# Sparse attention's top-k: the lower 16 bits of each threshold read from eight sorted values, with a branch to the bit search; two changes of queue order

## The chip, the cores and the metric

One core of one Trainium2 chip runs the whole program. The metric is the device time of one execution in microseconds. Matmuls run on TensorE (PE), the other work on VectorE (DVE), ScalarE (ACT) and GpSimd (POOL); SyncE (SP) and POOL issue the transfers between HBM and the on-chip memory. Each engine takes its instructions strictly in the order of its own queue, and semaphores join the queues.

## What is computed

Two layers over 1040 tokens (16 learned ones ahead of 1024) of width 1024: a mixer with a residual add, then a SwiGLU FFN. Layer 0 mixes by gated linear attention, layer 1 by sparse attention, cut here to what matters:

```python
def attend(args):                                   # 128 queries
    s_idx = einsum('bqhd,bsd->bqhs', qib, k_idx) * IDX_DIM ** -0.5
    score = einsum('bqhs,bqh->bqs', relu(s_idx), wb)       # the indexer: 8 heads of 64
    score = where(admissible[None], score, -inf)           # chunk-causal
    top_val, top_idx = lax.top_k(score, n_sel)             # n_sel = 256
    c_sel = c[top_idx]                                     # 256-wide latents
    q_lat = einsum('bqhd,hcd->bqhc', qb, w_uk)             # 8 heads of 128
    logits = einsum('bqhc,bqkc->bhqk', q_lat, c_sel) * ATT_HEAD_DIM ** -0.5 + bias
    u = einsum('bhqk,bqkc->bqhc', softmax(where(valid, logits, -inf)), c_sel)
    return einsum('bqhc,hcd->bqhd', u, w_uv)
```

All is float32. `lax.top_k` takes the earlier key among equal scores.

## The kernel before

A product of float32 operands is three matmuls (`mm3`, L230 to L232) of parts that `split` makes: a rounded high part (`xh`, a cast on ACT, L225) and the rest (`xl`, a subtraction on DVE or POOL, L226). Names like `xh`, `wl`, `cth` in rows are such parts.

**Top-k.** The kernel gathers no keys: it finds for each of 1024 queries the 256th largest score and adds a mask to the logits. The scores `sc` (L915 to L924) stand with 128 queries on the partitions in eight blocks of up to 1040 keys; block 0 needs no search, and blocks 7, 1, 4, 3 and 5, 2, 6 form the two groups of `GROUPS`. The threshold is found bit by bit: a score's float bits, made monotone, are two 16-bit halves. `rounds(15)` counts on the upper half, one bit in a step: for each block one instruction counts the keys below `cand` (three blocks on ACT, L1102, four on DVE, L1105), and four small POOL instructions in `decide` (L1114 to L1118) set the next `cand`. `turnover` then leaves in the mask's buffer the lower half of the keys whose upper half equals the threshold's, and 0 for the rest; its count (L1175) is of the keys above. `rounds(16)` searches the lower half in the same way, then `th` (L1165 to L1142) puts the bits back, and seven steps write the mask: L1207 to L1214, with a prefix sum (L1209) for the ties.

**What sets the order.** `topk` is a generator, and its steps are spread over `units` (L955 on), PE's work beside it: nine units of the latents (projection L1024, root L279, `turn` L1038 to transpose them), then queries `(hd, c)` of eight heads by three stretches of tokens (344, 344, 336), keys, values. `costs` weighs each step, and after every unit so many steps are emitted as their weights have earned. `later.at(d, f)` puts `f` off by `d` ticks, and each unit ends with one tick. After this, attention starts: POOL adds the mask to the bias (L1275), PE makes logits, DVE the softmax sums (L1290).

**Ahead of the indexer.** The last FFN group of layer 0 ends with `second`: for its last tokens five partial products (`EARLY`, on the first half of the hidden rows) are made before the eight whole ones, whose results are added to `h` (L728). `ended` gives the norm's root to `later` (L833); its row mean on PE is L323. Then `dsa` makes index keys (ps of 344), index queries of two stretches (384 and 512 wide, four pairs of heads `e`) and transposes of the head weights (L935).

## Time and profile before

| what | value |
|---|---|
| runs | 2595.59, 2597.05, 2598.44 us (median 2597.05) |
| profiled execution | 2597.97 us, its span 2596.2 us |
| granted TensorE clock over the span | 0.985 |

The rows below come from the profiled execution, its times counted from the start of the span. "Busy" is time in which an engine ran an instruction; a releaser in brackets is what ended the idle time before it. [...] Rows of DVE and ACT of consecutive instructions can overlap by some hundredths.

### The profile page before, as it was taken

Reading aid. Unit: us, or ns where it says so; the run is one execution under the profiler, and the core shown is the slowest. Engines: PE = TensorE matmul, PEld = TensorE weight load, DVE = VectorE, ACT = ScalarE, POOL = GpSimd, SP = SyncE. Lnnn points to the kernel's source line nnn. Section 1 sums busy time; section 2 is a strip of 40 time slices with the busy share of each in tenths; the row PEclk is TensorE's granted clock in tenths of the full one; section 3 lists DMA queues with packets and bytes.
Section 4 is the critical chain, followed back from the end, with each engine's and each line's share of the span. In section 5 each row is a group of like instructions: output and inputs, shape, how many; then the busy total and the mean of one; then the engine's idle time right before and its main releaser. Section 6 shows DMA issues by size and latency. Waiting matters only on the chain.

```text
span 2596.2 us, 37989 instructions
## 1 busy us (share of the span) xinstructions
PE 2515.9 (97%) x15096; PEld 2334.5 (90%) x15096; DVE 1356.1 (52%) x2904; ACT 955.3 (37%) x1972; POOL 382.2 (15%) x587
## 2 busy tenths in 40 slices
PE   7999999999999999999898969999999999999997
PEld 6999999999999999999878959999988888888887
DVE  7575566643333334444679997762633333333336
ACT  5764453521111111112568867761511111111114
POOL 3000000111111111110203455440200000000001
PEclk9999999999999999999899979999999999999999
DMA  3113013123333333332311101122111111111111
GB/s 119 41 35 108 26 49 115 33 86 122 122 115 117 111 122 110 112 116 72 111 65 53 63 25 42 64 95 86 39 60 49 49 49 49 49 42 41 48 49 66
DMA packets 68788, 190.00 MB, mean 73 GB/s; under 512 B 7065, under 2 KB 18609, under 8 KB 65794
## 3 DMA queue, kind: packets, MB, share of 16 engines
q1 hardware_dynamic: 62642, 154.31, 17.9%
q0 software_dynamic: 5968, 33.26, 3.8%
q8 instruction: 118, 1.93, 0.3%
q14 instruction: 60, 0.49, 0.1%
HBM read 150.74 MB, written 41.58 MB: 74 GB/s over the span
## 4 chain that ended last, share of the span: by engine, by line
PE 40%; DVE 6%; issue 2%; ACT 2%; POOL 1%; DMA 0%; POOLq 0%; ACTq 0%; DVEq 0%
PE ps L231 12%; PE ps L232 12%; PE ps L230 12%; DVE jd L1105 2%; PE ps L1322 1%; DVE sc L924 1%; PE ps L1334 1%; PE ps L915 1%; POOL xl L226 0%; PE ps L917 0%; DVE pre L1209 0%; DVE no L342 0%; PE ps L1310 0%; ACT L330 0%; DVE h L342 0%
## 5 line engine op out<-in xcount | busy, mean ns | idle before, releaser
L230 PE MATMUL ps<-xh,wh 128*128 128x344 f32 (+6 forms) x2808 | 945.5, 337 | 1.9 <-DMA wh<-s_qidx_h 1.2
L231 PE MATMUL ps<-xl,wh 128*128 128x344 f32 (+6 forms) x2808 | 941.6, 335 | 1.0 <-POOL xl L226 0.6
L232 PE MATMUL ps<-xh,wl 128*128 128x344 f32 (+6 forms) x2808 | 940.1, 335 | 1.9 <-DVE wl L197 1.9
L230 PEld LDWEIGHTS ps<-xh,wh 128*128 128x128 f32 x2808 | 528.5, 188 | 32.4 <-DMA wh<-s_qidx_h 1.3
L231 PEld LDWEIGHTS ps<-xl,wh 128*128 128x128 f32 x2808 | 528.8, 188 | 30.1 <-DVE xl L226 1.0
L232 PEld LDWEIGHTS ps<-xh,wl 128*128 128x128 f32 x2808 | 528.8, 188 | 29.2 <-DVE wl L197 2.5
L715 DVE TENSOR_TENSOR t<-sg,ps 128x344 f32<-128x344 f32 (+4 forms) x116 | 65.1, 562 | 639.6 <-PE ps L232 637.9
L192 ACT CAST wh<-wraw 128x1056 fp32r<-128x1056 f32 (+2 forms) x160 | 163.9, 1049 | 581.1 <-PE ps L231 573.3
L728 DVE TENSOR_TENSOR h<-h,ps 128x344 f32<-128x344 f32 (+3 forms) x456 | 251.1, 567 | 163.9 <-PE ps L232 163.7
L230 PE MATMUL ps<-hh,wh 128*128 128x512 f32 (+2 forms) x800 | 280.3, 350 | 0.0
L231 PE MATMUL ps<-hl,wh 128*128 128x512 f32 (+2 forms) x800 | 280.0, 350 | 0.0
L232 PE MATMUL ps<-hh,wl 128*128 128x512 f32 (+2 forms) x800 | 279.8, 350 | 0.0
L197 DVE TENSOR_TENSOR wl<-wraw,wh 128x1056 fp32r<-128x1056 f32 (+2 forms) x158 | 192.1, 1238 | 72.3 <-ACT wh L192 70.5
L230 PE MATMUL ps<-wh,xh 128*128 128x256 f32 (+9 forms) x560 | 174.4, 311 | 9.4 <-ACT xh L225 5.0
L232 PE MATMUL ps<-wh,xl 128*128 128x256 f32 (+9 forms) x560 | 169.6, 303 | 4.3 <-DVE xl L226 2.3
L714 ACT ACTIVATE sg<-ps 128x344 f32<-128x344 f32 (+4 forms) x116 | 57.8, 498 | 300.6 <-PE ps L232 295.6
L231 PE MATMUL ps<-wl,xh 128*128 128x256 f32 (+9 forms) x560 | 167.7, 299 | 0.0
L225 ACT CAST hh<-t 128x344 fp32r<-128x344 f32 (+4 forms) x116 | 60.0, 517 | 285.2 <-DVE t L715 285.2
L230 PEld LDWEIGHTS ps<-hh,wh 128*128 128x128 f32 x800 | 150.0, 188 | 14.6
L231 PEld LDWEIGHTS ps<-hl,wh 128*128 128x128 f32 x800 | 150.3, 188 | 14.3
L232 PEld LDWEIGHTS ps<-hh,wl 128*128 128x128 f32 x800 | 150.5, 188 | 13.9
L230 PEld LDWEIGHTS ps<-wh,xh 128*128 128x128 f32 x560 | 110.9, 198 | 15.5 <-ACT xh L225 5.6
(289 smaller groups left out, 3390.1 us busy)
## 6 DMA issues: line engine op xcount, KB each, us to landing
wraw<-in_w_fi SPq DMA_DIRECT2D x44, 528.0 KB, 3.9
wraw<-in_w_fi SPq DMA_DIRECT2D x44, 496.0 KB, 4.9
wraw<-in_w_fo SPq DMA_DIRECT2D x22, 528.0 KB, 3.9
wraw<-in_w_fo SPq DMA_DIRECT2D x22, 496.0 KB, 5.0
s_skew<-s_rel POOLq DMA_DIRECT2D x8, 583.5 KB, 13.7
h<-in_ht SPq DMA_DIRECT2D x8, 520.0 KB, 5.1
wraw<-s_skew SPq DMA_DIRECT2D x8, 520.0 KB, 3.5
sg<-in_w_dq SPq DMA_DIRECT2D x16, 256.0 KB, 4.1
```

The costliest lines, as they stand in the source:

```text
L192: nc.scalar.copy(hi[:, a:e], r[:, : e - a])
L197: self.wlow.tensor_sub(lo[:, c:d], r[:, c - a : d - a], hi[:, c:d].bitcast(F32))
L225: self.nc.scalar.copy(hi, src)
L230: mm(p, sh, mh, start=first, stop=False, skip_group_check=True)
L231: mm(p, sh, ml, start=False, stop=False, skip_group_check=True)
L232: mm(p, sl, mh, start=False, stop=last, skip_group_check=True)
L714: nc.scalar.activation(sg[:, :n], pg[:, :n], AF.Silu)
L715: v.tensor_mul(t[:, :n], sg[:, :n], pu[:, :n])
L728: v.tensor_add(self.h[:, d, a : a + n], self.h[:, d, a : a + n], p[:, :n])
L915: nc.tensor.matmul(p, qx[:, hd, t], kxh[:, s0 : s0 + n], start=True, stop=False)
L924: eng.scalar_tensor_tensor(o, rt, wx[:, b, hd : hd + 1], o, op0=OP.mult, op1=OP.add)
L1105: v.tensor_scalar(j[:, :n], mu(b), cand, None, op0=OP.is_lt, op1=OP.add, accum_out=out)
```

## The change

1. **Top-k.** `rounds(16)` goes. `turnover` counts by ACT sign counts (7 of them, L1201) in place of DVE's seven counts, takes the eight largest lower halves of each block (`v.max`, seven instructions), works out each row's rank among the equal keys, and picks the value of that rank by a mask over eight places. `worst` is the largest rank of all rows; a 1x1 matmul (L1251) sums over the partitions whether any rank is above 7.5, a flag goes to DVE's register (L1254), and DVE branches (L1256): with the flag set it runs `search`, the 16 bits on DVE alone; otherwise it jumps over it. `If` puts an unconditional branch on every other engine at that place.
2. **Costs.** The list of step weights is 66 times 1.7 before; now 32 times 1.7, two of 6, one of 3. The mask steps keep theirs.
3. **Latents.** `turn` is put off by two more ticks.
4. **Index queries.** The 512-wide ones of `e` 0 and 1 come ahead of the head weights' transposes and of the 384-wide ones of `e` 2 and 3 (those of 0 and 1 are made earlier, among the keys).
5. **FFN.** One more tick after the five early products, and the root of the last but one stretch put off by 3 ticks for 2.
6. Rows 0 to 63 of block 1 get a mask of zeros at the end (their 272 keys less the inadmissible are 208 and fewer than 256, all taken).

```diff
@@ -756,6 +756,7 @@
...
                                 done[e] = out(hh, hl, wo, e, *cs[c], qs=[0])
+                            later.tick()
@@ -829,7 +830,7 @@
...
-                self.later.at(2 if a == last_chunks[-2][0] else 1, rstd)
+                self.later.at(3 if a == last_chunks[-2][0] else 1, rstd)
@@ -926,18 +927,26 @@
...
+                def head_weights():
+                    p = self.ps()
+                    for b in range(8):
+                        a = META + 128 * b
+                        nc.tensor.transpose(p[:, b * 64 : b * 64 + 64], wt[64:128, a : a + 128],
+                                            self.ident[64:128, 64:128])
+                    v.tensor_scalar(wx, p.rearrange("p (b c) -> p b c", b=8)[:, :, 0:8], 8 ** -0.5,
+                                    0.125, op0=OP.mult, op1=OP.mult)
...
+                for e in range(2):
+                    index_queries(144, 384, e)
+                index_queries(528, 512, 0)
+                index_queries(528, 512, 1)
+                head_weights()
+                for e in range(2, 4):
+                    index_queries(144, 384, e)
                 for e in range(4):
-                    index_queries(144, 384, e)
-                    if e == 0:
...
-                for e in range(4):
-                    index_queries(528, 512, e)
+                    if e > 1:
+                        index_queries(528, 512, e)
@@ -952,7 +961,7 @@
...
-                costs = [1.7] * 66 + [MASK] * 8
+                costs = [1.7] * 32 + [6.0] * 2 + [3.0] + [MASK] * 8
@@ -1029,7 +1038,7 @@
...
-                self.later.at(3 + i % 3, lambda i=i, c=c: turn(i, c))
+                self.later.at(5 + i % 3, lambda i=i, c=c: turn(i, c))
@@ -1083,11 +1094,17 @@
...
+        place = pool.tile([128, 8], F32, name="place")
+        for i in range(8):
+            v.memset(place[:, i : i + 1], float(i))
+        worst = pool.tile([128, 2], F32, name="worst")
+        flag = pool.tile([1, 1], I32, name="flag")
@@ -1154,6 +1171,11 @@
...
+            for c, b in enumerate(g["b"]):
+                n = nkeys(b)
+                v.tensor_scalar(g["rest"][:, c : c + 1], g["thr"][:, c : c + 1], -0.5 if c < g["na"] else -1.0,
+                                -1.0 if c < g["na"] else n / 2 - 1.0, op0=OP.mult, op1=OP.add)
@@ -1166,33 +1188,74 @@
...
-        def turnover(g):
-            cand = g["cand"]
-            for c in list(range(g["na"], g["n"])) + list(range(g["na"])):
+        def turnover(g, j):
+            cand, n, na, x, rank = g["cand"], g["n"], g["na"], g["x"], g["rank"]
+            top = pool.tile([128, n, 8], U16, name="top%d" % j)
+            tops = pool.tile([128, n, 8], F32, name="tops%d" % j)
+            v.tensor_scalar_add(x, cand, 0.5)
+            for c in range(n - 1, -1, -1):
                 b = g["b"][c]
-                n, tc = nkeys(b), cand[:, c : c + 1]
-                j = pool.tile([128, T], BF16, name="jd", tag="pre", bufs=2)
-                v.tensor_scalar(j[:, :n], mu(b), tc, None, op0=OP.is_gt, op1=OP.add,
-                                accum_out=g["cnt"][:, c : c + 1])
-                low = pool.tile([128, T], U16, name="low", tag="sg", bufs=2)[:, :n]
+                m, tc = nkeys(b), cand[:, c : c + 1]
+                t = pool.tile([128, T], BF16, name="jd", tag="pre", bufs=2)
+                nc.scalar.activation(t[:, :m], mu(b), AF.Sign, bias=x[:, c : c + 1], scale=-1.0,
+                                     accum_out=g["cnt"][:, c : c + 1])
+                low = pool.tile([128, T], U16, name="low", tag="sg", bufs=2)[:, :m]
                 nc.scalar.activation(low, half(b, 0), AF.Identity, bias=g["add"][:, c : c + 1],
                                      scale=g["sgn"][:, c : c + 1])
                 v.scalar_tensor_tensor(mu(b), mu(b), tc, low, op0=OP.is_equal, op1=OP.mult)
-            more(g, g["cnt"])
+                v.max(out=top[:, c, :], in_=mu(b))
             bits_of(g, 1)
-            start(g, 16)
+            v.scalar_tensor_tensor(rank, g["cnt"], 0.5, g["rest"], op0=OP.mult, op1=OP.add)
+            if 1 in g["b"]:
+                v.memset(rank[0:64, g["b"].index(1) : g["b"].index(1) + 1], 0.0)
+            v.tensor_reduce(worst[:, j : j + 1], rank, axis=mybir.AxisListType.X, op=OP.max)
+            for c in range(n):
+                v.tensor_scalar(tops[:, c, :], place, rank[:, c : c + 1], None, op0=OP.is_equal)
+            v.tensor_tensor(tops, tops, top, op=OP.mult)
+            v.tensor_reduce(cand, tops, axis=mybir.AxisListType.X, op=OP.max)
+        def search():
+            for g in groups:
+                thr, cand, below, flip = g["thr"], g["cand"], g["below"], g["flip"]
+                for c, b in enumerate(g["b"]):
+                    v.tensor_scalar(thr[:, c : c + 1], g["rank"][:, c : c + 1], -1.0, nkeys(b) - 1.0,
+                                    op0=OP.mult, op1=OP.add)
+                start(g, 16)
+                for bit in range(15, -1, -1):
+                    for c, b in enumerate(g["b"]):
+                        n = nkeys(b)
+                        t = pool.tile([128, T], BF16, name="jd", tag="pre", bufs=2)
+                        v.tensor_scalar(t[:, :n], mu(b), cand[:, c : c + 1], None, op0=OP.is_lt,
+                                        op1=OP.add, accum_out=g["cnt"][:, c : c + 1])
+                    v.tensor_sub(below, g["cnt"], thr)
+                    v.tensor_scalar(below, below, 0.0, -(2.0 ** bit), op0=OP.is_gt, op1=OP.mult)
+                    v.tensor_add(cand, below, flip)
+                    if bit:
+                        v.tensor_scalar_add(flip, cand, 2.0 ** (bit - 2) if bit > 1 else 0.5)
         for g in groups:
             signs(g)
             yield
         yield from rounds(15)
+        for j, g in enumerate(groups):
+            decide(g, 0)
+            turnover(g, j)
+            yield
+        v.tensor_reduce(worst[:, 0:1], worst, axis=mybir.AxisListType.X, op=OP.max)
+        v.tensor_scalar(worst[:, 0:1], worst[:, 0:1], 7.5, None, op0=OP.is_gt)
+        p = self.ps()
+        nc.tensor.matmul(p[0:1, 0:1], worst[:, 0:1], self.mean[:, 0:1], start=True, stop=True)
+        v.tensor_scalar(flag, p[0:1, 0:1], 0.0, None, op0=OP.is_gt)
+        yield
+        many = nc.values_load(flag, engines=[mybir.EngineType.DVE], min_val=0, max_val=1,
+                              skip_runtime_bounds_check_because="a comparison gives zero or one")
+        with self.tc.If(many > 0):
+            search()
         for g in groups:
-            decide(g, 0)
-            turnover(g)
-            yield
-        yield from rounds(16)
-        for g in groups:
-            decide(g, 0)
             bits_of(g, 0)
             clamp(g, g["th"].bitcast(F32))
...
+            if b == 1:
+                v.memset(mk(b)[0:64, :], 0.0)
```

What the change moves, by the order of instructions (before and after are apart; a bracket names the engines or transfer queues waited for).

**PE at the indexer's begin**, the last index key product and what follows it, before:

```order
7946 L231 MATMUL ps<-xl,wh 128x344 [waits Pool_49]
7947 L232 MATMUL ps<-xh,wl 128x344
7948 L935 MATMUL ps<-ident,wt 128x64 [waits DMAHW2_49,DMAHW3_49,DMAHW0_49,DMAHW5_49,PE_49,Activation_49]
7949 L935 MATMUL ps<-ident,wt 128x64
7950 L935 MATMUL ps<-ident,wt 128x64 [waits Activation_49]
7951 L935 MATMUL ps<-ident,wt 128x64 x2
7952 L935 MATMUL ps<-ident,wt 128x64 [waits Activation_49]
7953 L935 MATMUL ps<-ident,wt 128x64 x2
7954 L230 MATMUL ps<-xh,wh 128x384 [waits DMASW2_49]
7955 L231 MATMUL ps<-xl,wh 128x384
```

Now, with 45 more matmuls of width 512 above these rows (48 in all between the keys and the transposes):

```order
7993 L230 MATMUL ps<-xh,wh 128x512
7994 L231 MATMUL ps<-xl,wh 128x512
7995 L232 MATMUL ps<-xh,wl 128x512
7996 L934 MATMUL ps<-ident,wt 128x64 [waits DMAHW2_49,DMAHW3_49,DMAHW0_49,DMAHW5_49,PE_49,Activation_49]
7997 L934 MATMUL ps<-ident,wt 128x64
7998 L934 MATMUL ps<-ident,wt 128x64 [waits Activation_49]
7999 L934 MATMUL ps<-ident,wt 128x64 x2
8000 L934 MATMUL ps<-ident,wt 128x64 [waits Activation_49]
8001 L934 MATMUL ps<-ident,wt 128x64 x2
8002 L230 MATMUL ps<-xh,wh 128x384 [waits DMASW2_49,DVE_49]
8003 L231 MATMUL ps<-xl,wh 128x384
```

The transposes of `wt` and the 384-wide products, which wait for a load (DMASW), have moved behind 48 matmuls of width 512 that wait for nothing.

**PE in the latents**, the last of 96 matmuls of width 256 and the first transposes, before, and the last of 144 now:

```order
8414 L230 MATMUL ps<-wh,xh 128x256
8415 L231 MATMUL ps<-wl,xh 128x256
8416 L232 MATMUL ps<-wh,xl 128x256
8417 L1038 MATMUL ps<-ident,qf 128x16 [waits DVE_49,Activation_49]
8418 L1038 MATMUL ps<-ident,qf 128x16
8419 L230 MATMUL ps<-wh,xh 128x256 [waits Activation_49]
```

```order
8463 L230 MATMUL ps<-wh,xh 128x256
8464 L231 MATMUL ps<-wl,xh 128x256
8465 L232 MATMUL ps<-wh,xl 128x256
8466 L1047 MATMUL ps<-ident,qf 128x16 [waits DVE_49,Activation_49]
8467 L1047 MATMUL ps<-ident,qf 128x16
8468 L230 MATMUL ps<-wh,xh 128x256 [waits PE_49]
```

Two more units of 24 matmuls stand ahead of the first transposes. **ACT at the same place**, the last mask of `signs` and the root of the latents' norm, before and now:

```order
787 L1159 ACTIVATE mask<-sc,add_13507,sgn_13506 128x784
788 L1102 ACTIVATE ja,cnt_13481<-mask,cand_13485 128x1040 [waits Activation_49]
789 L1102 ACTIVATE ja,cnt_13481<-mask,cand_13485 128x272 [waits Activation_49]
790 L279 ACT_TABLE_LOAD
791 L279 ACTIVATE rs<-rs 128x3 [waits DVE_49]
792 L1102 ACTIVATE ja,cnt_13500<-mask,cand_13504 128x784 [waits Activation_49]
793 L1102 ACTIVATE ja,cnt_13481<-mask,cand_13485 128x1040 [waits Activation_49,Pool_49]
```

```order
786 L1181 ACTIVATE mask<-sc,add_13520,sgn_13519 128x784
787 L279 ACT_TABLE_LOAD
788 L279 ACTIVATE rs<-rs 128x3 [waits DVE_49]
789 L1119 ACTIVATE ja,cnt_13492<-mask,cand_13496 128x1040 [waits Activation_49]
790 L1119 ACTIVATE ja,cnt_13492<-mask,cand_13496 128x272 [waits Activation_49]
791 L1033 ACTIVATE qf,css<-ps 128x256 [waits PE_49]
792 L1119 ACTIVATE ja,cnt_13513<-mask,cand_13517 128x784 [waits Activation_49]
```

The root has moved ahead of two counts.

**PE in the queries** now, the end of unit (6,1) and the begin of (7,1); ahead of these rows stand the 72 matmuls of (6,0), (7,0) and (6,1), after them 24 of (7,1), 48 of width 336, then keys:

```order
9033 L230 MATMUL ps<-xh,wh 128x344
9034 L231 MATMUL ps<-xl,wh 128x344
9035 L232 MATMUL ps<-xh,wl 128x344
9036 L1251 MATMUL ps<-mean,worst 1x1 [waits DMAHW3_49,DMAHW4_49,DMAHW2_49,DMAHW6_49,DMAHW1_49,DMAHW7_49,DVE_49,Activation_49]
9037 L230 MATMUL ps<-xh,wh 128x344 [waits Activation_49]
9038 L231 MATMUL ps<-xl,wh 128x344
9039 L1256 UNCONDITIONAL_BRANCH
9040 L232 MATMUL ps<-xh,wl 128x344
```

**DVE at the thresholds**, the end of the search before, and now, with the rows of `search` (L1225 to L1236) between:

```order
1522 L226 TENSOR_TENSOR xl<-qf,xh 128x3x344 [waits Activation_49]
1523 L1105 TENSOR_SCALAR jd,cnt_13500<-mask,cand_13504 128x400 [waits DVE_49,Pool_49]
1524 L1105 TENSOR_SCALAR jd,cnt_13500<-mask,cand_13504 128x912 [waits DVE_49]
1525 L1165 TENSOR_TENSOR cand_13485<-cand_13485,sgn_13487 128x4 [waits Activation_49,Pool_49]
1526 L1166 TENSOR_TENSOR cand_13485<-cand_13485,add_13488 128x4 [waits DVE_49]
1527 L1167 CAST th_13489<-cand_13485 128x4 [waits DVE_49]
1528 L1140 SCALAR_TENSOR_TENSOR x_13490<-th_13489 128x4 [waits DVE_49]
1529 L1141 TENSOR_SCALAR y_13491<-x_13490 128x4 [waits DVE_49]
1530 L1142 TENSOR_TENSOR th_13489<-th_13489,y_13491 128x4 [waits DVE_49]
1531 L1165 TENSOR_TENSOR cand_13504<-cand_13504,sgn_13506 128x3 [waits Activation_49,Pool_49]
1532 L1064 SCALAR_TENSOR_TENSOR xl<-ps,xh 128x336 [waits Activation_49] x2
```

```order
1472 L1249 TENSOR_SCALAR worst<-worst 128x1 [waits DVE_49]
1473 L1218 TENSOR_REDUCE cand_13517<-tops_14766 128x3 [waits DVE_49]
1474 L226 TENSOR_TENSOR xl<-qf,xh 128x3x344 [waits Activation_49]
1475 L1073 SCALAR_TENSOR_TENSOR xl<-ps,xh 128x344 [waits Activation_49] x2
1476 L1252 TENSOR_SCALAR flag<-ps 1x1 [waits PE_49]
1477 L1254 TENSOR_LOAD flag [waits DMAHW3_49,DMAHW2_49,DMAHW4_49,DMAHW1_49,DMAHW5_49,DMAHW0_49,DMAHW6_49,DVE_49,DMAHW7_49,Activation_49,Pool_49]
1478 L1256 COMPARE_AND_BRANCH
1479 L1225 TENSOR_SCALAR thr_13494<-rank_13503 128x1 x4
1723 L1236 TENSOR_TENSOR cand_13517<-below_13516,flip_13518 128x3 [waits DVE_49]
1724 L1256 UNCONDITIONAL_BRANCH
1725 L1256 UNCONDITIONAL_BRANCH [waits DVE_49]
1726 L1187 TENSOR_TENSOR cand_13496<-cand_13496,sgn_13498 128x4 [waits DVE_49]
```

The thresholds (`cand` to `th`) followed the last decision of POOL; now they follow the branch, and so do the parts of the second stretch of queries (`xl` from `qf`), which stood ahead of them.

## Rows read from the trace of the kernel before

**Rows 1.** Page, part 1: each engine's busy time, share of the span, instructions.
```profile
PE 2515.9 (97%) x15096; PEld 2334.5 (90%) x15096; DVE 1356.1 (52%) x2904; ACT 955.3 (37%) x1972; POOL 382.2 (15%) x587
```

**Rows 2.** Windows: stretch, its length, then busy us (instructions) per engine; TensorE's granted clock.
```profile
1242.00:1246.00 4.00, 0.86 (x3) 0.50 (x2) 2.99 (x7) 2.74 (x5) 1.09 (x2) 0.78 0.78 245
1246.00:1252.00 6.00, 6.00 (x24) 5.72 (x23) 1.39 (x3) 3.79 (x5) 0.00 (x0) 0.58 0.99 329
1282.00:1286.00 4.00, 1.49 (x12) 1.14 (x10) 2.87 (x6) 2.54 (x6) 1.07 (x2) 0.90 0.33 96
1286.00:1292.00 6.00, 4.26 (x13) 3.71 (x14) 1.24 (x3) 0.52 (x2) 0.00 (x0) 0.50 0.73 289
1340.00:1360.00 20.00, 19.70 (x77) 11.29 (x76) 20.00 (x43) 18.49 (x39) 0.00 (x0) 1.00 0.01 2
1378.00:1386.00 8.00, 0.86 (x8) 0.66 (x6) 5.00 (x17) 7.97 (x14) 2.26 (x9) 0.88 0.00 1
1386.00:1392.00 6.00, 5.70 (x31) 5.69 (x32) 5.97 (x17) 5.06 (x17) 2.70 (x12) 0.59 0.01 1
1400.00:1490.00 90.00, 90.00 (x583) 89.94 (x582) 88.47 (x231) 75.82 (x172) 43.12 (x184) 1.00 0.20 71
1490.00:1545.00 55.00, 29.45 (x139) 26.27 (x138) 52.33 (x131) 32.69 (x81) 28.12 (x51) 0.75 0.06 20
```

**Rows 3.** Waits of PE: waiting line, releaser, us in total, times, longest.
```profile
PE ps L230 <- DVE xl L1064: 10.6, 2, 6.5
...
PE ps L1038 <- ACT ja L1102: 7.4, 1, 7.4
```

**Rows 4.** Timeline of PE: start, us, instruction, idle before it and releaser.
```profile
1245.31 1.52 PE L323 MATMUL ps<-na,mean 128*128 128x344 f32 x2 [3.14 <-DVE na L304]
...
1286.58 0.58 PE L935 MATMUL ps<-ident,wt 64*128 64x64 f32 x3 [3.10 <-ACT wt L893]
```

**Rows 5.** Timeline of DVE, first residual add after the early down matmuls.
```profile
1251.65 1.96 DVE L728 TENSOR_TENSOR h<-h,ps 128x344 f32<-128x344 f32 x4 [1.25 <-PE ps L232]
```

**Rows 6.** Timeline of ACT, between the latents' masks and the root.
```profile
1380.46 1.15 ACT L1102 ACTIVATE ja<-mask,cand 128x1040 bf16<-128x1040 uint16 x1
...
1382.23 1.28 ACT L279 ACT_TABLE_LOAD   x1
```

**Rows 7.** Timeline of PE, queries: first 344-wide and first 336-wide of four units.
```profile
1469.42 0.32 PE L230 MATMUL ps<-xh,wh 128*128 128x344 f32 x1
...
1484.53 0.32 PE L230 MATMUL ps<-xh,wh 128*128 128x336 f32 x1
```

**Rows 8.** Timeline of DVE: one bit's first count, the next bit's, and thresholds.
```profile
1457.31 0.89 DVE L1105 TENSOR_SCALAR_CACHE_REDUCE jd<-mask,cand 128x656 bf16<-128x656 uint16 x1
...
1460.45 0.89 DVE L1105 TENSOR_SCALAR_CACHE_REDUCE jd<-mask,cand 128x656 bf16<-128x656 uint16 x1
...
1508.44 0.16 DVE L1165 TENSOR_TENSOR cand<-cand,sgn 128x4 f32<-128x4 f32 x1 [0.82 <-POOL cand L1116]
```

**Rows 9.** Costliest groups of DVE, 1370 to 1545 us: count, busy, mean ns, idle before.
```profile
L1209 DVE TENSOR_TENSOR_SCAN pre<-mask 128x272 f16<-128x272 bf16 (+6 forms) x7 | 10.5, 1525 | 0.0
...
L1175 DVE TENSOR_SCALAR_CACHE_REDUCE jd<-mask,cand 128x656 bf16<-128x656 uint16 (+6 forms) x7 | 5.9, 890 | 0.0
...
L226 DVE TENSOR_TENSOR xl<-qf,xh 128x1032 fp32r<-128x1032 f32 (+1 forms) x3 | 4.3, 1438 | 0.0
...
L1064 DVE SCALAR_TENSOR_TENSOR xl<-ps,xh 128x344 fp32r<-128x344 f32 (+1 forms) x6 | 2.8, 506 | 0.0
...
L1165 DVE TENSOR_TENSOR cand<-cand,sgn 128x4 f32<-128x4 f32 (+1 forms) x4 | 0.6, 160 | 0.9 <-POOL cand L1116 0.8
```

**Rows 10.** Page, parts 3 and 6: the instruction queue; one weight load's landing time.
```profile
q8 instruction: 118, 1.93, 0.3%
...
wraw<-in_w_fo SPq DMA_DIRECT2D x22, 496.0 KB, 5.0
```

More of the change, by code (lines that the diff above doesn't have):

```diff
@@ L927, in score @@
                         v.memset(sc[0:64, off[b + 1] - 64 : off[b + 1]], SENTINEL)
-                for e in range(4):
-                    index_queries(144, 384, e)
-                    if e == 0:
-                        p = self.ps()
-                        for b in range(8):
-                            a = META + 128 * b
-                            nc.tensor.transpose(p[:, b * 64 : b * 64 + 64], wt[64:128, a : a + 128],
-                                                self.ident[64:128, 64:128])
-                        v.tensor_scalar(wx, p.rearrange("p (b c) -> p b c", b=8)[:, :, 0:8], 8 ** -0.5,
-                                        0.125, op0=OP.mult, op1=OP.mult)
-                for e in range(4):
-                    index_queries(528, 512, e)
+                def head_weights():
[13 more added lines that the diff above has]
+                    index_queries(144, 384, e)
+                for e in range(4):
+                    if e > 1:
+                        index_queries(528, 512, e)
                     for b in range(1, 4):
@@ L1089, in topk @@
             for name, dt in (("cnt", F32), ("all", F32), ("thr", F32), ("below", F32), ("cand", F32),
-                             ("flip", F32), ("sgn", F32), ("add", F32), ("th", I32), ("x", F32), ("y", F32)):
+                             ("flip", F32), ("sgn", F32), ("add", F32), ("th", I32), ("x", F32), ("y", F32),
+                             ("rank", F32), ("rest", F32)):
                 g[name] = pool.tile([128, g["n"]], dt, name=f"{name}{j}")
```

## The prediction

> **What bounds the kernel now.** I read the page first: PE is busy for 97% of the span and no other engine for more than 52% [rows 1]. So the time is PE's own work plus the places where PE waits or runs at its lower clock, and the question is how much of that loss the change takes away. Next I cut the stretch of the indexer and the top-k into windows [rows 2]. A full-rate measure is the window 1400:1490: 583 matmuls in 90.00 us at clock 1.00, so 0.154 us each at a width near 344. Three stretches fall short of it. At the indexer's begin, 1242:1252 and 1282:1292, PE gets few instructions done and the clock falls to 0.58 and 0.50. In the latents, 1378:1392, PE is busy for 0.86 of 8 us and then runs at 0.59. At the top-k's end, 1490:1545, it is busy for 29.45 of 55 us while DVE is busy for 52.33. The waits of PE say for whom [rows 3]: 10.6 us in two waits for DVE's `xl` of L1064, which stands behind the bit search, and 7.4 us for ACT in the latents. The scores (1340:1360) have DVE full, 20.00 of 20, and nothing here touches them.
>
> **The FFN's early products.** PE's row mean L323 waits 3.14 us for DVE [rows 4], with 15 ready matmuls of the early products queued behind it. They now stand ahead of it. Run at full rate they take 15 x 0.154 = 2.3 us of the wait; in the window behind it the 24 matmuls take 0.25 us each [rows 2], so 15 cost 3.75 us there. The gain lies between these, as far as the first residual add at 1251.65 [rows 5] waits for PE and not for the norm; I take 3.5. The same edit in layer 1 and the norm's root a tick later I cost at nothing: the root's result is wanted only after the eight whole products, and if that cover is gone a tick is one product, 24 x 0.154 = 3.7 us.
>
> **The index queries.** The head weights' transposes wait 3.10 us for ACT's copy [rows 4], and behind them the 384-wide products wait for their weights. In 1282:1286 PE does 12 instructions and in 1286:1292 it does 13, worth 1.8 and 2.0 us at full rate, so 2.2 + 4.0 = 6.2 us are lost. Now 48 ready matmuls 512 wide stand there; scaled from 0.154 us by width that is 48 x 0.23 = 11 us of work, more than the whole loss. DVE's scores begin one unit later in PE's order, but DVE is full only later (1340:1360), so I cost that at nothing; if PE has to wait for DVE to drain the two sets of scores that now come together, it takes back part of it, down to nothing gained. Both edits together: A = 3.5 + 6.2 = 9.7, between 4 and 10.
>
> **The latents' turn.** At full rate a 256-wide matmul takes 0.154 x 256 / 344 = 0.115 us. The 8 and 31 instructions of 1378:1386 and 1386:1392 are then worth 0.9 and 3.6 us: 7.1 + 2.4 = 9.5 us are lost. Two more units put 48 x 0.115 = 5.5 us of work into the wait of 7.4. Besides, ACT's root moves ahead of two counts that took it from 1380.46 to 1382.23 [rows 6], 1.8 us. Together 7.3, so the wait is nearly filled: B = 8.5, between 5 (the wait's rest stays and the clock falls again) and 9.5. So PE comes to the last queries s = A + B = 18.2 us earlier (9 to 19.5).
>
> **The search.** Sixteen bits go, at 1460.45 - 1457.31 = 3.14 us each [rows 8]: 50 us of DVE's time. It does not come out as 50, because of where the branch now stands. PE's 1x1 matmul L1251 is queued behind unit (6,1). Four units take 1484.53 - 1469.42 = 15.11 us [rows 7], 3.78 each; behind three of them PE is there at 1480.75 - s = 1462.5. DVE's `worst` is ready before that: without the search at about 1508.44 - 50.2 = 1458.2, less A, 1448.5. The additions lie in this gap of 14 us. MAX8 is not in the trace; it reads each element once, so I bound it from below by the seven counts that it replaces (5.9 us, L1175) and from above by the seven scans (10.5, L1209) [rows 9]: 0 to 4.6 us more. Some 20 small instructions at 0.16 [rows 9] make 3.2. That ends by about 1456. Were PE at L1251 before that, each further us of s would be lost here.
>
> From L1251 on there is a serial piece, X: the flag on DVE, the load into the register, the branch, and code from behind the jump. No row shows such a load or a jump. From below it is a few small instructions, 1 us; from above two transfers one behind the other, 5.0 us each by the landing time of a weight load [rows 10], so 10. Code does come by transfers here (118 packets of queue 8). The jump passes some 246 rows of `search`, so I take one such transfer: X = 5.
>
> [...]
>
> Behind the branch come the thresholds, at 1508.44 before [rows 8] and now at 1462.5 + 5 = 1467.5, so 40.9 us earlier. From there DVE has masks, splits of queries and keys, and softmax sums until 1545, and it is full (52.33 of 55 us): this tail stays as long as it was, and its end moves with its begin. It grows by the second stretch's `xl` (1.44) and L1064's pair (2 x 0.51) [rows 9], 2.4 us that were done ahead of the thresholds and now stand behind the branch. So the end of the tail moves by 40.9 - 2.4 = 38.5 us, of which s is a part: 25.3 + s - X. All behind it is as before. From the profiled execution's 2597.97: **2559.5 us**. That execution is 0.9 above the median of the runs, which is within their spread, and I leave it.
>
> **The rivals.**
> *The tail is hidden too.* If DVE, started 41 us earlier, no longer delays keys and logits, PE is bound by its own work. Its loss in the tail is 55 - 139 x 0.154 = 33.6 us; all of it and s give 51.8, so 2546. For it: PE waits there for named pieces of DVE. Against it: DVE has 36 us of work behind the thresholds, and PE has only 72 query matmuls (11 us), keys and values to lay beside them.
> *The waits only move.* The scores' or the latents' gain is partly lost (s = 12) and the branch costs two fetches (X = 10): 25.3 + 12 - 10 = 27, so 2571; with s = 9 and more behind the branch 2575 or so. For it: DVE's load of the flag waits for every engine and for the transfers issued before it, and one late piece there holds all of DVE.
> *Slower: the search runs.* If one row needs the ninth or a later value among its equals, the flag is set and DVE does 16 bits x (5.9 us of seven counts [rows 9] + 8 small at 0.16) = 115 us in front of the tail: 2559.5 + 115 = 2674. It decides from a rank of 8 on. Worked out in float32 from the reference's inputs, the largest rank of any row is 7, in one row; the kernel's sums are made in another order, so one row could tip over, but only there.
> *No change.* The load could wait for something that ends with the old thresholds, and A and B be swallowed by DVE's full scores: X near 40, a time near 2595.
>
> **How the numbers follow.** The forecast has 0.62, its own range 2551 to 2569 (s from 14 to 19.5, X from 1 to 10). The hidden tail has 0.12, the moved waits 0.19, the search 0.04, no change 0.03. A range of 2546 to 2573 holds the forecast, half and more of the hidden tail and over half of the moved waits: about 0.8. A measurement of this kernel can tell about 0.2%, 5 us, from no change; all cases but the last two are faster by more, 0.93; within it 0.03; slower 0.04.
>
> **What would show it.** PE's row mean L323 without its 3.1 us wait, and PE at the higher clock in the 10 us around the head weights; the first transposes of the latents with a wait under 2 us; about 14 us of idle DVE ahead of the flag; from PE's 1x1 matmul to `th` about 5 us; no count of `search` in the rows; then a DVE tail of 36 to 39 us at nearly full, with PE waiting for some 15 to 20 us in it. The prediction is wrong if `th` comes much later than 5 us behind the 1x1 matmul, if that matmul is late because PE waits for `worst`, or if PE's waits in the tail vanish or grow.

## The result and the profile after

| | before | after |
|---|---|---|
| median of 4 runs, us | 2596.94 (2595.59 to 2598.44) | 2560.14 (2557.45 to 2560.66) |
| profiled execution, its span, us | 2597.97, 2596.2 | 2560.66, 2558.9 |
| granted clock over the span | 0.985 | 0.992 |

The ratio is 0.986, its 95% interval 0.9846 to 0.9874: faster by 1.4%, clear of the runs' spread; 36.8 us by the medians and 37.3 us by the spans of the profiled executions, where 38.5 were forecast. The first part of after's profile page answers to [rows 1]; DVE has lost 46 us of work, PE's share has grown:

```profile
PE 2506.4 (98%) x15098; PEld 2325.8 (91%) x15098; DVE 1310.1 (51%) x2798; ACT 917.9 (36%) x1890; POOL 354.7 (14%) x461
```

The windows of after (columns of [rows 2]) show where PE still falls short:

```profile
1252.00:1264.00 12.00, 10.38 (x51) 8.11 (x49) 9.09 (x19) 7.60 (x14) 3.09 (x3) 0.95 0.34 118
1264.00:1270.00 6.00, 5.73 (x19) 5.32 (x19) 5.08 (x11) 2.18 (x6) 2.10 (x2) 0.54 0.00 0
1282.00:1292.00 10.00, 10.00 (x49) 7.88 (x47) 2.81 (x5) 2.86 (x6) 0.48 (x1) 1.00 0.54 206
1370.00:1386.00 16.00, 14.67 (x117) 14.09 (x117) 14.06 (x48) 15.29 (x41) 6.48 (x25) 1.00 0.04 7
1450.00:1460.00 10.00, 10.00 (x66) 10.00 (x65) 0.48 (x1) 2.02 (x4) 0.06 (x1) 1.00 0.01 2
1481.00:1513.00 32.00, 22.07 (x116) 19.27 (x115) 31.88 (x72) 17.03 (x45) 14.89 (x12) 0.84 0.12 35
```

The index queries (1282:1292) and the latents (1370:1386) now run at clock 1.00. In the index keys (1264:1270) PE, which waits in pieces for the norm's splits, runs mostly at the lower clock, 0.54; before has such a stretch too, some microseconds later and shorter:

```profile
1266.00:1272.00 6.00, 4.69 (x16) 4.18 (x17) 4.37 (x9) 3.37 (x7) 1.93 (x3) 0.72 0.00 0
```

The tail (1481:1513) has DVE full, 31.88 of 32, and PE does 116 matmuls there, worth at most 116 x 0.154 = 17.9 us, since about half of them are only 256 wide. Of PE's waits [rows 3] the one for ACT in the latents is gone and the two for `xl` are down from 10.6 to 1.7; the waits that remain in these stretches are short:

```profile
PE ps L230 <- DVE wl L226: 2.8, 3, 1.4
PE ps L230 <- DVE big L1319: 2.6, 1, 2.6
...
PE ps L323 <- DVE na L304: 1.8, 2, 1.1
PE ps L230 <- DVE xl L1073: 1.7, 1, 1.7
...
PE ps L230 <- DVE qf L1039: 1.3, 1, 1.3
```

The chain around the branch, first PE's timeline at the 1x1 matmul, then DVE's:

```profile
1464.20 0.32 PE L232 MATMUL ps<-xh,wl 128*128 128x344 f32 x1
1464.45 0.19 PE L1251 MATMUL ps<-mean,worst 128*1 128x1 f32 x2
1464.57 0.42 PE L230 MATMUL ps<-xh,wh 128*128 128x344 f32 x1
```

```profile
1445.30 0.15 DVE L1249 TENSOR_SCALAR worst<-worst 128x1 f32<-128x1 f32 x1
...
1459.52 1.24 DVE L226 TENSOR_TENSOR xl<-qf,xh 128x1032 fp32r<-128x1032 f32 x1 [13.95 <-ACT xh L225]
1461.01 0.94 DVE L1073 SCALAR_TENSOR_TENSOR xl<-ps,xh 128x344 fp32r<-128x344 f32 x2 [0.26 <-ACT xh L1072]
1464.67 0.15 DVE L1252 TENSOR_SCALAR flag<-ps 1x1 int32<-1x1 f32 x1 [2.72 <-PE ps L1251]
1468.76 0.23 DVE L1187 TENSOR_TENSOR cand<-cand,sgn 128x4 f32<-128x4 f32 x2 [3.94 <-DVEq L1256]
```

PE reaches L1251 without a wait; `worst` has been ready for 19 us, and DVE has stood idle for 13.95 and 2.72 us. From the 1x1 matmul to the thresholds 4.3 us pass, 3.94 of them idle ahead of the first instruction behind the branch (DVEq is DVE's sequencer). The thresholds come at 1468.76, 39.7 us before those of [rows 8].

I follow every kernel below by three landmarks: the 1x1 matmul, the thresholds (L1187 or its like), and the next keys' first matmul behind the tail, which in after is:

```profile
1535.45 0.41 PE L230 MATMUL ps<-cth,uh 128*128 128x352 f32 x1
```

| kernel | us (median, or one run) | 1x1 | thresholds | next keys | thresholds to keys |
|---|---|---|---|---|---|
| before | 2596.94 | none | 1508.44 | 1571.33 | 62.9 |
| after | 2560.14 | 1464.45 | 1468.76 | 1535.45 | 66.7 |
| turn_back | 2564.35 | 1469.28 | 1473.62 | 1540.32 | 66.7 |
| index_back | 2565.39 | 1469.52 | 1473.88 | 1540.56 | 66.7 |
| ffn_back | 2562.28 | 1464.84 | 1469.40 | 1536.11 | 66.7 |
| topk_only | 2571.85 | 1473.97 | 1478.31 | 1545.01 | 66.7 |
| short_body | 2556.29 (one) | 1462.96 | 1465.02 | 1531.71 | 66.7 |
| flag_early | 2560.89 | 1453.37 | 1457.70 | 1534.76 | 77.1 |
| flag_pairs | 2561.56 | 1455.11 | 1459.46 | 1536.05 | 76.6 |

The last column of the first six kernels with the branch is the same to 0.03 us: one chain, from PE's queue over the branch into DVE's tail. For differences of the other columns between two kernels there is a limit: already at L323, which waits for DVE's `na` with the edits and without them, the profiled executions stand between 1243.80 (topk_only) and 1245.42 (flag_early), so a landmark can differ by up to 1.6 us from one execution to the next.

### The profile page after: what moved, and what is told of

The parts are those of the page before. It is cut to its first block, busy times and chain, and to the rows that moved or that the text cites. A ratio compares the mean times of both kernels' runs of the same rounds, so it can differ in the third digit from the quotient of the medians.

```text
span 2558.9 us, 37579 instructions
## 1 busy us (share of the span) xinstructions
PE 2506.4 (98%) x15098; PEld 2325.8 (91%) x15098; DVE 1310.1 (51%) x2798; ACT 917.9 (36%) x1890; POOL 354.7 (14%) x461
## 5 line engine op out<-in xcount | busy, mean ns | idle before, releaser
L230 PE MATMUL ps<-xh,wh 128*128 128x344 f32 (+5 forms) x2808 | 946.9, 337 | 1.7 <-DVE qf L1039 1.3
L231 PE MATMUL ps<-xl,wh 128*128 128x344 f32 (+5 forms) x2808 | 943.0, 336 | 1.6 <-POOL xl L226 1.0
L232 PE MATMUL ps<-xh,wl 128*128 128x344 f32 (+5 forms) x2808 | 941.9, 335 | 1.9 <-DVE wl L197 1.9
## 6 DMA issues: line engine op xcount, KB each, us to landing
s_skew<-s_rel POOLq DMA_DIRECT2D x8, 583.5 KB, 14.2
```

Of the source, the lines that this page charges most:

```text
L230: mm(p, sh, mh, start=first, stop=False, skip_group_check=True)
L231: mm(p, sh, ml, start=False, stop=False, skip_group_check=True)
L232: mm(p, sl, mh, start=False, stop=last, skip_group_check=True)
```

## The experiments

**The parts undone one at a time, and the top-k alone.** `turn_back` has the turn's ticks as before, `ffn_back` the FFN's, `index_back` the order of the index queries; `topk_only` has all three. The lines of the three edits, cut short and with the label behind the first of each:

```diff
-                self.later.at(5 + i % 3, lambda i=i, c=c: turn(i, c))     # turn_back
+                self.later.at(3 + i % 3, lambda i=i, c=c: turn(i, c))
-                            later.tick()                                  # ffn_back
-                self.later.at(3 if a == last_chunks[-2][0] else 1, rstd)
+                self.later.at(2 if a == last_chunks[-2][0] else 1, rstd)
-                for e in range(2):                                        # index_back
-                    index_queries(144, 384, e)
-                index_queries(528, 512, 0)
...
+                for e in range(4):
```

> The changed kernel with the latents' transposes at their old place (two ticks sooner). Theory of one chain (PE's queue up to the 1x1 matmul, then 4.3 us to the thresholds, then a DVE tail of fixed length): the 7.9 us that PE gained in the latents come back one for one, the 1x1 matmul stands near 1472 us and the time is 2568 us. Rival (the tail absorbs it, since DVE idles for 14 us ahead of the flag): 2560 to 2562 us.

> The changed kernel without the extra tick after the early products and with the norm's root one tick sooner, in both layers. One chain: the layer-0 part is worth what is left of it behind the index keys, 2.8 us, and the layer-1 part at the very end 1.5 us: 2564.4 us. Rival 1 (only the 15 matmuls moved into the wait count, nothing in layer 1): 2562.4 us. Rival 2 (the 4.4 us seen at the first index keys all reach the end, and 1.5): 2566 us.

> The changed kernel with the index queries in their old order, the head weights' transposes first. One chain: the 5.7 us that PE gained between the second index keys and the latents come back: 2565.8 us, the 3 us wait for the copied weights and the clock of 0.5 behind it are there again. Rival (DVE is full in the scores and swallows what comes before): 2560 to 2561 us.

> The kernel before with the top-k change and the step costs alone; the FFN, the index queries and the latents as they were. One chain: PE is at the 1x1 matmul at 1480.8 us, thresholds 4.3 us later at 1485.1, 23.4 us sooner than before, of which the longer tail takes 3.8: a gain of 19.6 us, 2577.5 us. Rival (the removed search alone decides, 50 us of DVE work, so that all of PE's loss of 34 us in the tail goes): 2563 us.

Ratios to before: turn_back 0.9878 (0.9861 to 0.9894), ffn_back 0.9874 (0.9857 to 0.9890), index_back 0.9883 (0.9866 to 0.9899), topk_only 0.9913 (0.9896 to 0.9929). Over after's median they cost 4.2, 2.1, 5.3 and together 11.7 us. By the 1x1 matmul the turn is worth 4.8, the index queries 5.1, the FFN 0.4, the three together 9.5, and each moves the thresholds and the next keys by as much, to 0.3 us. Counted from L323 in each execution (1245.21, 1244.57, 1245.08, 1243.80, and 1245.19 in after) they are 4.8, 5.7, 0.5 and together 10.9, so the parts add up.

Of the expectations, index_back came as said (2565.8) and ffn_back at its first rival (2562.4). turn_back cost 3.7 us less than its 2568, since the top-k's edits had shortened the wait already, and topk_only came 5.7 below its 2577.5: its 1x1 matmul stands at 1473.97 and not at 1480.8.

The waits come back where they were. PE's waits of turn_back, the timeline of index_back at the head weights, and its window there:

```profile
PE ps L1047 <- ACT ja L1119: 5.0, 1, 5.0
```

```profile
1282.64 0.58 PE L936 MATMUL ps<-ident,wt 64*128 64x64 f32 x3 [2.84 <-ACT wt L894]
```

```profile
1282.00:1288.00 6.00, 4.00 (x12) 3.43 (x13) 1.24 (x3) 0.58 (x2) 0.00 (x0) 0.50 0.77 309
```

The latents' wait is 5.0 here and not the 7.4 of [rows 3]: the top-k's edits, with the root ahead of two counts, had shortened it by 2.4 without the turn (in topk_only it is 4.95 too). In ffn_back the mean waits as before and the first index key comes 3.1 us later than in after, but the latents only 0.4 us later. The PE rows, ffn_back's and then after's:

```profile
1245.08 1.36 PE L323 MATMUL ps<-na,mean 128*128 128x344 f32 x2 [3.15 <-DVE na L304]
...
1254.95 0.32 PE L230 MATMUL ps<-xh,wh 128*128 128x352 f32 x1
```

```profile
1245.19 0.85 PE L323 MATMUL ps<-na,mean 128*128 128x344 f32 x2 [0.77 <-DVE na L304]
...
1251.85 0.33 PE L230 MATMUL ps<-xh,wh 128*128 128x352 f32 x1
```

Keys that start 3.1 us earlier then wait for splits of the norm, which come only 2.1 earlier (DVE's last one for them at 1264.40 for 1266.49). After's PE rows in the keys:

```profile
1261.44 0.42 PE L231 MATMUL ps<-xl,wh 128*128 128x344 f32 x1 [0.55 <-DVE xl L226]
1263.11 0.65 PE L231 MATMUL ps<-xl,wh 128*128 128x344 f32 x1 [0.56 <-POOL xl L226]
```

The first 384-wide index query behind the keys still starts 1.7 us earlier (1266.56 for 1268.26), but there the clock of after has fallen and that of ffn_back has not: from these queries to the next keys after takes 9.77 us at 0.85, ffn_back 8.40 at 1.00, and 0.3 us are left. The windows around, ffn_back's and then after's, have PE equally busy, for fewer matmuls in after:

```profile
1256.00:1282.00 26.00, 24.22 (x130) 21.56 (x129) 18.47 (x36) 15.15 (x30) 9.97 (x11) 1.00 0.11 34
```

```profile
1256.00:1282.00 26.00, 24.12 (x113) 21.18 (x112) 17.96 (x35) 15.11 (x31) 10.01 (x11) 0.87 0.04 10
```

The 2.1 us between the medians of after and ffn_back lie within overlapping intervals.

**The orders alone.** The kernel before, with the FFN, index and turn edits and the old search:

```diff
+                            later.tick()
...
+                index_queries(528, 512, 0)
+                index_queries(528, 512, 1)
+                head_weights()
...
-                self.later.at(3 + i % 3, lambda i=i, c=c: turn(i, c))
+                self.later.at(5 + i % 3, lambda i=i, c=c: turn(i, c))
```

> The kernel before with the changes of order alone (FFN tick, index queries, latents' turn), the bit search as it was. One chain: DVE's search starts behind the scores and sets the thresholds, so only what lies ahead of the scores counts, 5 to 6 us (the index queries' 5.3 and some tenths of the FFN): 2591 us, and the latents' 4 to 5 us are waited away in front of the keys. Rival (the edits add up wherever they lie): 5.3 + 0.4 + 4.2, so 2587 us.

2587.2 us (2586.87 to 2588.61, six runs), 0.9965 (0.9953 to 0.9978): the number of the rival, 2587, and not the 2591 of the chain. The latents start 9.1 us earlier than before (1356.43 for 1365.48) and PE's last stretch of queries, 336 wide, 11.0 earlier (1473.49 for 1484.53), but the thresholds only 7.9:

```profile
1500.58 0.16 DVE L1174 TENSOR_TENSOR cand<-cand,sgn 128x4 f32<-128x4 f32 x1 [0.82 <-POOL cand L1125]
```

With the search in DVE's queue the thresholds follow DVE and POOL, not PE, and of s only what brings the search forward counts. The same edits are worth 11.7 us with the branch and 8 to 9 with the old search; by the spread of the runs these two are barely apart.

**The search, run in every execution.** The limit on `worst` is made -1, so the flag is always set.

```diff
-        v.tensor_scalar(worst[:, 0:1], worst[:, 0:1], 7.5, None, op0=OP.is_gt)
+        v.tensor_scalar(worst[:, 0:1], worst[:, 0:1], -1.0, None, op0=OP.is_gt)
```

> The changed kernel with the bound on the rank at -1 instead of 7.5, so that the flag is always set and DVE runs the search. As forecast for the slower rival: 16 bits of seven counts and eight small instructions, 115 us in front of the tail, 2675 us, with the thresholds near 1584 us. Rival (small instructions hide in each other's latency, and the fetch behind the jump goes): 16 x 6.5 - 3 = 101 us, 2661 us.

2671.71 us, one run, where the rival in the prediction said 2674 and the expectation 2675. DVE's timeline, from the flag to the search and behind it:

```profile
1462.87 0.15 DVE L1252 TENSOR_SCALAR flag<-ps 1x1 int32<-1x1 f32 x1 [2.73 <-PE ps L1251]
1464.10 0.42 DVE L1225 TENSOR_SCALAR thr<-rank 128x1 f32<-128x1 f32 x5 [1.08 <-issue]
...
1580.53 0.23 DVE L1187 TENSOR_TENSOR cand<-cand,sgn 128x4 f32<-128x4 f32 x2
```

The search takes 1580.53 - 1464.10 = 116.4 us (115 were worked out). With the branch not taken 1.08 us pass ahead of the next instruction; taken, 3.94. So after, which has no row of the search, jumps over it, and the jump itself costs about 2.9 us.

**The jump made short.** The body of the branch is cut to one bit in place of sixteen, some 20 rows to jump over; a search in it would be incomplete, but the flag is never set here.

```diff
-                for bit in range(15, -1, -1):
+                for bit in range(0, -1, -1):
```

> The changed kernel with a search of one bit instead of sixteen in the branch's body (some 20 rows in place of 246); the body isn't run, so what it leaves out is not missed. Theory (the 2.9 us between the taken jump and the thresholds are the fetch of code that lies out of reach): from the 1x1 matmul to the thresholds 1.5 us instead of 4.3, about 2557 us. Rival (a taken jump costs this at any distance): 4.3 us again, 2560 us.

DVE's rows:

```profile
1463.19 0.14 DVE L1252 TENSOR_SCALAR flag<-ps 1x1 int32<-1x1 f32 x1 [2.73 <-PE ps L1251]
1465.02 0.23 DVE L1187 TENSOR_TENSOR cand<-cand,sgn 128x4 f32<-128x4 f32 x2 [1.68 <-DVEq L1256]
```

1.68 us for 3.94: the length of the jump costs 2.3 us, and the thresholds to keys stay 66.7. (The one run is 3.9 us below after; 1.2 of that stand at L323 already, 1243.95 for 1245.19, and have nothing to do with the jump.) The instruction queues point to a fetch of code in these 2.3 us. In after one packet of an instruction queue, of 8 KiB, lies between the compare-and-branch (1465.8) and the thresholds; it starts at 1466.84. The DMA view of the window 1465.8:1468.7:

```profile
q14 instruction: 1, 0.01, 0.7%
```

turn_back and topk_only have such a packet at the same place, 2.4 us behind the 1x1 matmul. short_body has none from its compare-and-branch (1464.3) to its thresholds (1465.02). It is not queue 8, which the prediction looked at [rows 10], and the trace does not name the engine that a packet is for. That DVE waits for this packet is inferred from its place, and from the run without one; no row shows the wait itself. In after the register load took 0.545 us and the compare-and-branch 0.07.

**No branch.** The flag, the 1x1 matmul, the branch and the search are left out; the thresholds stand directly behind the ranks.

```diff
-        nc.tensor.matmul(p[0:1, 0:1], worst[:, 0:1], self.mean[:, 0:1], start=True, stop=True)
-        v.tensor_scalar(flag, p[0:1, 0:1], 0.0, None, op0=OP.is_gt)
...
-        with self.tc.If(many > 0):
-            search()
```

> The changed kernel without flag, 1x1 matmul, branch and search: what it leaves out is the search for rows with a rank above 7, which these inputs don't have. One chain: the thresholds follow the turnover at about 1446 us, 22 us sooner, and the tail moves by 20 until PE's own work binds it: of the 22 us that PE loses in the tail now it gets back 15 to 18, so 2543 us. Rival (the place of the branch costs little, the tail is bound elsewhere): 2555 us or more.

2552.04 us, ratio 0.983 (0.9814 to 0.9847): 8.1 us below after, between the 2543 expected and its rival's 2555. The thresholds come at about 1444.5, 24 us earlier than in after, but the next keys only 8.0 (1527.42). From the thresholds to the next keys 82.9 us pass for after's 66.7; DVE is idle for 14.2 of them (3.8 in after) and busy for 5.8 more. PE, busy for 76.2 of the 82.9, has two waits for DVE in this tail, and neither is for a mask:

```profile
1482.08 0.39 PE L230 MATMUL ps<-uh,cth 128*128 128x256 f32 x1 [0.94 <-DVE xl L1073]
...
1488.37 0.58 PE L230 MATMUL ps<-uh,cth 128*128 128x256 f32 x1 [4.62 <-DVE wl L226]
```

**The flag brought forward.** `flag_early` lowers the two costs of 6 and the 3 and spreads the masks, so that the 1x1 matmul comes 11 us earlier; `flag_pairs` has the early flag too, with other weights for the masks, and issues each mask behind the last splits of a pair of queries (L1073). The edit of flag_early:

```diff
-                costs = [1.7] * 32 + [6.0] * 2 + [3.0] + [MASK] * 8
+                costs = [1.7] * 32 + [3.5] * 2 + [1.0] + [3.5] * 8
```

> The changed kernel with step costs that bring the turnover and the 1x1 matmul earlier in PE's queue, behind unit (5,2) instead of (6,1), 72 matmuls sooner. One chain: worst is ready at 1445 us and the 1x1 matmul runs at 1453 instead of 1464.5; the thresholds come 11.4 us sooner, and the first stretch's splits (2.2 us) now fall behind them: a gain of 9 us, 2551 us. Rival 1 (worst comes later, as its steps are squeezed together, and PE waits for it): 2556 us or more. Rival 2 (PE has no more to gain in the tail): 2560 us.

> The early flag again (1x1 matmul behind unit (5,2)), with other step costs and with each mask step put behind the last split of a query pair (L1073), so that PE's keys and values no longer wait for three masks. One chain with PE's own work as its floor: thresholds at 1457.7 us as with the early flag, the last query pair's split near 1477 instead of 1483, and a gain like that of the kernel without a branch, 8 us: 2552 us. Rival 1 (the DVE tail keeps its 66.7 us from the thresholds on): 2549 us. Rival 2 (an early flag gives nothing, whatever the order): 2560 us.

Neither gains over after: 2560.89, 0.9866 (0.985 to 0.9883), and 2561.56, 0.9865 (0.9849 to 0.9882). In flag_early the thresholds come 11.1 us earlier, the next keys 0.7. DVE now has all masks ahead of the last queries' `xl`, and PE stands:

```profile
1495.54 0.58 PE L230 MATMUL ps<-uh,cth 128*128 128x256 f32 x1 [12.00 <-DVE xl L1073]
```

With the order repaired (flag_pairs) the 12 us go, but DVE waits 1.4 to 2.0 us at each stretch for the queries that PE has yet to make, and the end is the same, as the second rival of its expectation said.

**Before, once more,** as a measure of spread.

> The kernel before, unchanged, for a second trace. Theory (the 4.4 us at the first index keys and 1.5 us at the very end are mostly differences between two executions, as the run without the FFN edit suggests): first index keys at 1253.5 to 1255 us instead of 1256.2, and a span 1 to 2 us shorter than 2596.2. Rival (the FFN edit gave them): 1256.2 and 2596.2 within 0.3 us.

2598.55 us, one run: latents at 1365.84 (before 1365.48), thresholds 1509.04, but the first index key at 1254.74 and not 1256.21. Executions of one kernel differ by 1.5 us there and agree again 100 us later. The clock does this: it falls in both, but in 1242:1256 the granted clock is 0.76 in the first and 0.88 in the second, in 1256:1280 it is 0.93 and 0.86. The span, 2596.8, is not shorter, as expected, but 0.6 longer.

**POOL kept off DVE's tail.** In after DVE's prefix sums are longer than in [rows 9], a mean of 1789 ns for 1525, 12.5 us for 10.5. `quiet_pool` gives the splits of the second and third stretch of queries to DVE in place of POOL.

```diff
-                    if j in QPOOL:
+                    if j in QPOOL and c == 0:
```

> The changed kernel with the splits of heads 3 to 5 for the second and third stretch of queries on DVE instead of POOL. Theory (DVE's mask instructions take longer while POOL runs): the 272-wide scan takes 0.72 us instead of 1.35, the others that lay beside those splits likewise; DVE gets 2.5 us more work and loses less than that in stretched instructions: 2560 to 2562 us. Rival (their length has another reason): the 272-wide scan takes 1.35 us again.

The sums by shape, after's and then quiet_pool's:

```profile
L1272 DVE TENSOR_TENSOR_SCAN pre<-mask 128x784 f16<-128x784 bf16 x1 | 2.9, 2859 | 0.0
...
L1272 DVE TENSOR_TENSOR_SCAN pre<-mask 128x272 f16<-128x272 bf16 x1 | 1.4, 1350 | 0.0
```

```profile
L1272 DVE TENSOR_TENSOR_SCAN pre<-mask 128x784 f16<-128x784 bf16 x1 | 1.8, 1778 | 0.0
...
L1272 DVE TENSOR_TENSOR_SCAN pre<-mask 128x272 f16<-128x272 bf16 x1 | 0.7, 725 | 0.0
```

Both are back at the lengths of before (1759 and 714 ns). In after the sum of 272 starts at 1472.07, beside POOL's splits (1471.02 to 1474.15), which quiet_pool takes away. The one of 784 has no split beside it. It starts at 1489.26, in the middle of an addition of a mask to the bias on POOL:

```profile
1489.03 1.44 POOL L1340 TENSOR_TENSOR sc<-wraw,mask 128x656 f32<-128x656 f32 x1 [1.94 <-DVE mask L1279]
```

In quiet_pool that addition is over, at 1489.95, when the sum starts at 1490.46. In no_branch the order is turned round: there the sum of 784 starts first (1458.06, an addition on POOL at 1458.24), takes 1.79 us, and it is POOL's addition of 656 that takes 2.86. The tail of quiet_pool is 65.7 in place of 66.7, though DVE has 2.5 us more to do in it. 2558.72 us, one run, lies among after's own runs, so it isn't a faster version that I could show. Why an instruction of one engine takes longer beside the other's no row shows.

## Why the prediction was right, by its own steps

The time, 2560.14 for 2559.5, and the mechanism were right. Three terms were mis-sized, and they partly cancel. (Of the prediction's own range the lower end, 2551, does not come out of its terms: s = 19.5 and X = 1 give 2554.)

- **What sets the thresholds** (PE's 1x1 matmul, not DVE): right. About 14 us of idle DVE were named as a sign, and 13.95 in one piece (and 2.72) measured; that these agree is luck. The prediction's own sum has `worst` ready by 1456 and PE at 1462.5, which leaves 6.5. `worst` was ready at 1445.3, 10.7 us ahead of the bound of 1456. Of that, 4.6 is MAX8: seven took 5.9 us, as much as the seven counts they replaced [rows 9], the lower bound; the rest I didn't trace, since nothing waited for it.
- **s = 18.2: measured 16.3.** Unshifted, the 1x1 matmul would have stood at 1480.75 [rows 7]; it came at 1464.45. A was 8.5 (latents at 1356.95 for 1365.48; 9.7 forecast) and B 7.8 (the rest; 8.5 forecast).
  - *FFN, 3.5:* the step that failed. The mean's wait went as said (3.14 to 0.77 in its row), and 3.1 us were there at the first index key, but the prediction gave the keys behind it no price at all: they wait for the norm's splits, which come 2.1 us earlier, and the 384-wide queries behind them run at a clock of 0.85. 0.4 us reached the latents. The root's later tick, put at nothing, is undone in ffn_back together with the rest, so its own part isn't shown.
  - *Index queries, 6.2:* nearly right. By index_back they are worth 5.0 at the latents, but its execution came to the second index keys, ahead of the edit, 0.9 us before after's (1275.43 for 1276.33); from there to the latents 86.6 us become 80.6.
  - *The turn, 8.5:* 4.8 from the two units (5.5 forecast). The wait's other 2.4 us go with the top-k's edits, the root among them (1.8 forecast); that it is the root alone was not tried.
  - A has 2.2 us left over (8.5 less 0.4 and 5.9), and topk_only, with neither of the edits there, starts the latents 3.8 us earlier than before (1361.67); 1.5 of these stand at L323 already. The rest is the clock. From L323 to the second index keys before takes 33.8 us and before_again 33.9, topk_only and ffn_back, with the same PE work there, 31.5 and 31.6, while PE is idle for 1.5 to 1.8 us of it in all four; in 1242:1280 the granted clock is 0.87 in the first two and 0.96 in the others. Two executions on each side don't show whether the top-k's edits bring that about or chance; no term of the prediction stands for it, so that A came as near as it did is in part luck.
- **X = 5: measured 4.3,** of which 2.3 hang on the length of the jump. One fetch was the right picture (one packet of 8 KiB lies there), the price of a weight load [rows 10] too high for it.
- **The tail is fixed and grows by 2.4:** fixed, yes, for thresholds as early as here or later (66.7 in six kernels); brought 9 to 11 us further forward it is 76.6 and 77.1. It grew by 3.8. Prefix sums beside POOL account for 2.0 us of longer DVE instructions; the rest isn't traced. DVE was as full as said, 38.1 of the 38.2 us behind the thresholds.
- **The sum.** 38.5, less 1.9 (s), plus 0.7 (X), less 1.4 (tail), is 35.9, which is what the next keys show (1571.33 - 1535.45). The spans differ by 37.3: 1.4 us more come in the rest of the span, where no edit but the FFN's stands. It is not that edit: the rest takes 1024.9 us in before and 1023.4 in after, but 1023.7 and 1023.6 in ffn_back and topk_only, which have the FFN as before, and down to 1022.7 in kernels that have after's. It is within what executions differ by.
- **The rivals.** The hidden tail (2546) shows itself in no_branch and the early flags: DVE started 24 us earlier gives 8, 9 to 11 us earlier gives nothing, and DVE waits for PE's queries instead. The moved waits happened in small, in the index keys. The search's price, 115, was 116.4.

PE is still short in the tail, by at least 32 - 17.9 = 14 us in 1481:1513, where the prediction said 15 to 20. An earlier flag doesn't give it back.

## What to carry to other kernels

When a long piece of work is taken off one engine, look for the instruction on another engine that the new order makes it wait for, and price the gain from there: here 50 us of DVE's search alone were worth some 23 (topk_only, 0.9913), since the flag stands in PE's queue, and 37 with the edits that bring PE to the flag earlier. Gains ahead of such a point counted one for one as long as the point was on the chain (topk_only against after: 9.5 us at the 1x1 matmul, 9.6 at the next keys); past it the next waits take them (flag_early: thresholds 11.1 us earlier, next keys 0.7, a wait of PE for DVE of 12.00). Work moved into a wait is worth the wait only if the work behind it has its operands: of the FFN's 3.1 us all but 0.4 were lost within 25 us, in waits for the norm's splits and at the lower clock behind them (0.85).

## What the runs showed of the hardware

- A branch on DVE, from the 1x1 matmul to the first instruction behind it: 4.3 us taken over some 246 rows, with one packet of an instruction queue in it; 2.1 us over some 20, with none. In after the parts were the flag 0.15, the register load 0.545, the compare-and-branch 0.07, and the idle time.
- MAX8 of 16-bit keys took 1.10 us at 912 and 0.57 at 400, about what a count with the same width takes in before (1.16 and 0.62): 1.0 ns for each further key in both.
- A prefix sum of 784 keys that started behind a POOL instruction still at work took 2.86 us, and 1.78 alone; one of 272 keys 1.35 and 0.73. Started just ahead of POOL's addition, a sum of 784 took 1.79, and the addition 2.86 in place of 1.44.
- The same PE work, from the row mean to the second index keys, took 33.8 and 33.9 us at a granted clock of 0.87 and 31.5 and 31.6 at 0.96.
